# The experts' ranking, in ten steps between the first blocks' work, behind the gates of the first quad

## The chip, the cores and the metric

The kernel runs on one core of a Trainium2 chip. The metric is the device time of one execution, in microseconds (us); lower is better. The engines of a core are named as in the profile: PE (TensorE, matrix products; PEld is its loading of the stationary operand), DVE (VectorE), ACT (ScalarE), POOL (GpSimd) and SP (SyncE, which here issues the loads of weights). Each engine works through a row of instructions of its own, in a fixed order, and waits on semaphores for what others produce.

## The reference

Two layers of a small diffusion transformer, then a last block. Each of the two layers has a mixer (convolutions in layer 0, attention in layer 1), and then a mixture of 32 experts, over 512 tokens in layer 0 and 256 in layer 1. What matters here is the mixture:

```python
def hier_moe(tokens, w1, b1, w2, b2, w_gate, w_up, w_down):
    n = tokens.shape[0]
    p1 = jax.nn.softmax((tokens @ w1 + b1).astype(jnp.float32), axis=-1)
    p_grp, grp = lax.top_k(p1, 1)                       # one of 4 groups
    lg2 = (tokens @ w2 + b2).astype(jnp.float32).reshape(n, N_GROUPS, EXPERTS_PER_GROUP)
    lg2 = jnp.take_along_axis(lg2, grp[:, :, None], axis=1)[:, 0]
    top_val, top_idx = lax.top_k(lg2, TOP_K_INNER)      # two of its 8 experts
    gate = p_grp * jax.nn.softmax(top_val, axis=-1)
    expert = grp * EXPERTS_PER_GROUP + top_idx
    return grouped_experts(tokens, expert, gate.astype(tokens.dtype), w_gate, w_up, w_down)
```

`grouped_experts` computes, for each token and each of its two experts e, `(silu(x @ w_gate[e]) * (x @ w_up[e])) @ w_down[e]`, scales it with the gate and adds it to the token. The model width is 1024, an expert's hidden width 512, all in float32: an expert has three matrices of 2 MB.

## The kernel before

**Slots and blocks.** Every expert gets a block of slots for its tokens (64 slots, or with two blocks of 32 more for the experts with most tokens). The plan of blocks is fixed when the kernel is built; which expert takes which place in it is found out as the kernel runs. The first four experts (`FIX`) keep their fixed places. The other 28 are ranked by their number of tokens in `order` (L1464). Two blocks of 64 slots make a pair (128 slots), two pairs a quad (256 slots); layer 0 has 7 quads, layer 1 has 5.

**`order`** is a chain of operations on DVE alone, over arrays of 28 x 28 on all 128 partitions: comparing the counts, summing to ranks, then (L1499) casting `rows`, the row numbers in memory of the 28 experts in their rank order; then the places (`base`, `place`, `cap`, `rest`), then each token's slot (`slots`), and at its end `gB`, the gate weights by place for all quads but the first. The first quad's gate weights `gA` don't depend on it. Its scratch memory shares a buffer with `ysb`, the output of the blocks' down products (tag "ysb", one buffer).

**The stream of weights.** SP issues the loads in one order into a ring of slots. A slot is filled again when PE has finished with what was in it. The fixed experts' loads stand at L298; those of ranked experts at L309, and ahead of each ranked gate matrix SP reads the expert's row number from `rows` (L305).

**The work on a quad.** `new` and `onehot` make the matrix OH that says which token is in which slot; `dispatch` collects the tokens of a quad into `xs` (products with OH into a PSUM tile `pd`). `gates(q)` multiplies OH with `gA` or `gB`, so that each slot has its gate weight, as four products per pair in layer 0 (two halves each in the trace's count) into one `pd` tile; DVE copies the columns that matter into `gs`. There are two PSUM buffers for `pd`. Then for each block `hidden` (32 products for gate and up, ACT's Silu and DVE's `g<-acc,gs,g`, which takes the gate weight `gs`), `turn` (PE transposes `g` into `pt`), `down` (products with the down matrix into `acc`, then ACT and DVE write `ysb`), and per pair `spread` (products `pd<-OT,ysb` and DVE's addition to `res`).

**The order of work.** Everything is put into a queue with a lead of two jobs, so that a job's products stand on PE two jobs ahead of its elementwise work. Each job taken from the queue also advances background work (`self.bg`), a list of generators that run a step at a time between the jobs; `blocks`, which counts overflowing blocks, is such a one (by `slowly`). `job` puts a function into the queue. In the program before, `order` ran in one piece where it is called, ahead of the first `hidden`, and the queued `gates(0)` partly ahead of it and partly behind.

Of the kernel before, what the change touches and what calls it, by code (L numbers as in the profile page):

```python
# [138 lines left out]
class Kernel:  # L139
# [18 lines left out]
    def build_stream(self):  # L158
# [29 lines left out]
        def experts(l):  # L188
# [6 lines left out]
            ends.append(len(st))  # L195

        experts(0)
        mod(ada[1], [1])
        aw = I["attn_w_in"][0]
# [8 lines left out]
        for h in range(2):  # L208
# [3 lines left out]
                       [(slice(0, P), slice(4, 8), kp(aw[512:1024], h * 512, 512))]))  # L212
        mod(ada[1], [5])
        experts(1)
        mod(wm, [0, 1])
        w2 = I["w_in_2"][0]
# [1247 lines left out]
    def order(self, ep, l, T, rt):  # L1464

        nc = self.nc
        n = NE - FIX
        tmp = ep.tile([P, 2048], F32, tag="ysb", bufs=1, name="order")  # L1470
        o = [0]

        def part(n):
            o[0] += n
            return tmp[:, o[0] - n:o[0]]

        def square(v):
            return v.rearrange("p (a b) -> p a b", a=n)

        def along(v):  # L1480
            return v.unsqueeze(1).to_broadcast([P, n, n])

        def across(v):
            return v.unsqueeze(2).to_broadcast([P, n, n])

        E, w = part(n * n), part(n * n)
        key, rank, f = (part(n) for _ in range(3))
        base, place, cap, u = (part(NE) for _ in range(4))
        io, cnt, rest = self.c("iota"), rt["cnt"], rt["rest"]
        ranks, bases = (rt["plan"][:, 256 + i * n:256 + (i + 1) * n] for i in range(2))  # L1490
        self.stt(key, cnt[:, FIX:NE], float(NE), io[:, 0:n], OP.mult, OP.subtract)
        self.tt(square(w), along(key), across(key), OP.is_gt)
        nc.vector.tensor_reduce(out=rank, in_=square(w), axis=AX.X, op=OP.add)

        self.tt(square(E), across(ranks), along(rank), OP.is_equal)
        self.tt(square(w), square(E), along(io[:, 0:n]), OP.mult)
        nc.vector.tensor_reduce(out=f, in_=square(w), axis=AX.X, op=OP.add)
        self.ts(f, f, float(P), OP.mult, float((l * NE + FIX) * P), OP.add)
        nc.vector.tensor_copy(rt["rows"][:, 0:n], f)  # L1499
        self.ext[l] = rt["rows"]  # L1500
        self.st_fill()

        ET = E.rearrange("p (a b) -> p b a", a=n)
        self.tt(square(w), ET, along(bases), OP.mult)
        nc.vector.tensor_reduce(out=base[:, FIX:NE], in_=square(w), axis=AX.X, op=OP.add)
        self.tt(square(w), ET, along(io[:, FIX:NE]), OP.mult)
        nc.vector.tensor_reduce(out=place[:, FIX:NE], in_=square(w), axis=AX.X, op=OP.add)
        self.ts(base[:, 0:FIX], io[:, 0:FIX], float(SLOTS), OP.mult)
        nc.vector.tensor_copy(place[:, 0:FIX], io[:, 0:FIX])
        m32, m64 = PLANS[l].more  # L1510
        self.ts(cap, io[:, 0:NE], 0.0, OP.mult, float(SLOTS), OP.add)
        c = cap[:, FIX:NE]
        self.ts(c, rank, float(m32), OP.is_lt, 32.0, OP.mult)
        self.ts(u[:, 0:n], rank, float(m64), OP.is_lt, 32.0, OP.mult)
        self.stt(c, c, 32.0, u[:, 0:n], OP.add, OP.add)
        self.tt(rest, cnt, cap, OP.subtract)

        T2 = 2 * T
        oh, tm, eq = (w[:, i * T2 * NE:(i + 1) * T2 * NE].rearrange("p (t n) -> p t n", t=T2) for i in range(3))
        v = part(T * NE).rearrange("p (t n) -> p t n", t=T)  # L1520
        pl = part(T2)
        fi, wts = (rt[k].rearrange("p i t -> p (i t)") for k in ("fi", "wts"))
        self.tt(oh, io[:, 0:NE].unsqueeze(1).to_broadcast([P, T2, NE]), fi.unsqueeze(2).to_broadcast([P, T2, NE]),
                OP.is_equal)
        self.tt(v, rt["posm"], cap.unsqueeze(1).to_broadcast([P, T, NE]), OP.is_ge)
        self.stt(v, v, 65536.0, rt["posm"], OP.mult, OP.add)
        self.tt(v, v, base.unsqueeze(1).to_broadcast([P, T, NE]), OP.add)
        for i in range(2):
            ts = slice(i * T, (i + 1) * T)
            self.tt(tm[:, ts], oh[:, ts], v, OP.mult)  # L1530
        nc.vector.tensor_reduce(out=rt["slots"], in_=tm, axis=AX.X, op=OP.add)
        self.tt(tm, oh, place.unsqueeze(1).to_broadcast([P, T2, NE]), OP.mult)
        nc.vector.tensor_reduce(out=pl, in_=tm, axis=AX.X, op=OP.add)
        self.tt(eq, io[:, 0:NE].unsqueeze(1).to_broadcast([P, T2, NE]), pl.unsqueeze(2).to_broadcast([P, T2, NE]),
                OP.is_equal)
        self.tt(tm, eq, wts.unsqueeze(2).to_broadcast([P, T2, NE]), OP.mult)
        self.tt(rt["gB"], tm[:, 0:T], tm[:, T:T2], OP.add)

    def blocks(self, ep, l, T, rt):

        nc = self.nc

        nbt = ep.tile([P, NE], F32, name="nbt")
        nbf = ep.tile([P, 2 * T], F32, name="nbf")
        for j in range(2 * T):
            self.ts(nbt, rt["rest"], float(j * SLOTS), OP.is_gt)
            nc.vector.tensor_reduce(out=nbf[:, j:j + 1], in_=nbt, axis=AX.X, op=OP.add)
            if j % 2:
                yield
        nc.vector.tensor_reduce(out=nbt[:, 0:1], in_=nbf, axis=AX.X, op=OP.add)  # L1550
        nc.vector.tensor_copy(rt["nb"], nbt[:, 0:1])

    def experts(self, ep, mp, l, T, hhl, rt):
# [8 lines left out]
        B = plan.blocks  # L1562
        NB = len(B)
        npair = (plan.slots + P - 1) // P
        nq = (plan.slots + 255) // 256
        pairs = [[i for i in range(NB) if B[i][1] // P == p] for p in range(npair)]
# [67 lines left out]
        def down(b):  # L1634

            e, off, m, first, last = B[b]
            us = slice(off % P, off % P + m)
            c = D * m // P

            def pe(k, n):  # L1640
                if k == 0:
                    st["y"] = self.acc()
                a = st["y"]
                w, num = st["wd", e]
                hT = st["hT", b].rearrange("p (k s) -> p k s", k=4)
                for i in range(k, k + n):
                    for j in range(P // m):
                        self.mm(a[j * m:(j + 1) * m, 0:c], hT[:, i], w[:, i, j * c:(j + 1) * c], i == 0, i == 3)
                if k + n == 4:
                    if last:  # L1650
                        self.done(num)
                    out(a)

            def out(a):
                if off % P == 0:
                    st["ysb"] = ep.tile([P, 2, D], F32R, tag="ysb", bufs=1, name="ysb")
                H, L = (st["ysb"][us, i] for i in range(2))

                H, L = (v.rearrange("s (k p) -> s k p", k=8) for v in (H, L))
                for ps in (lo, hi) if m == 64 else quarters:  # L1660
                    self.parts(H[:, :, ps], L[:, :, ps], a[ps, 0:c].rearrange("s (p k) -> s k p", k=8))

            return [(None, lambda _, a=a: pe(*a)) for a in (((0, 2), (2, 2)) if m == 64 else ((0, 4),))]

        def slots(p):

            return min(P, plan.slots - p * P)

        def gates(q):

            src = rt["gB" if q else "gA"]
            pd = self.pd()
            gs = st["gs", q] = ep.tile([P, 8], F32, tag="gs", bufs=2, name="gs")
            for p in range(2 * q, min(2 * q + 2, npair)):
                r, m = p % 2, slots(p)
                e0, e1 = B[pairs[p][0]][0], B[pairs[p][-1]][0] + 1
                for t in range(T):
                    self.mm(pd[0:m, 8 * r:8 * r + e1 - e0], self.OH[:, t, r * P:r * P + m].bitcast(F32),
                            src[:, t, e0:e1], t == 0, t == T - 1)
                for b in pairs[p]:  # L1680
                    e, off, m, _, _ = B[b]
                    c = 8 * r + e - e0
                    for i in range(P // m):
                        nc.vector.tensor_copy(gs[i * m:(i + 1) * m, nth[b]:nth[b] + 1],
                                              pd[off % P:off % P + m, c:c + 1])
# [43 lines left out]
        def job(f, *a):  # L1729
            self.push(None, lambda _: f(*a))  # L1730
# [17 lines left out]
        for p in range(npair):  # L1748
            o, q = at[pairs[p][0]], p // 2
# [24 lines left out]
        new(0)  # L1774
        for k in (0, 2, 4, 6):
            dispatch(st["xs", 0], k, 0, False)
        job(gates, 0)
        self.order(ep, l, T, rt)
        self.bg.append(self.slowly(self.blocks(ep, l, T, rt), 20, 1))
        for b in range(NB):  # L1780
            if l and B[b][0] == TABLES and B[b][3]:
# [1142 lines left out]
```

## Time and profile before

| | us |
|---|---|
| median of 3 runs | 1979.12 |
| lowest and highest run | 1971.8, 1981.99 |
| the profiled execution | 1978.93 |
| its span in the trace | 1977.2 |

The span is the part of the execution that the hardware profiler saw; what lies around it is 1.7 us. Mean granted clock of TensorE over the span: 0.922 of full speed, where 1 is 2.4 GHz. A row of the profile gives the start in us from the span's start, the duration, the engine, the line of the kernel, the operation, the tiles (out<-in), and in brackets the idle time of the engine just before with what released it.

### The profile page before, as it was taken

The page shows a single profiled execution, that of the slowest core. Times are in us where ns is not written, and L with a number is a line of the kernel's source. Part 1 is how long each engine was busy: PE and PEld are TensorE (multiplying, and loading weights), DVE is VectorE, ACT ScalarE, POOL GpSimd, SP SyncE. Part 2 cuts the span into 40 slices and gives each one's busy share as a digit, 9 for nine tenths or more (in the row PEclk, how much of TensorE's full clock was granted, in tenths as well). Part 3 has the DMA queues.
Part 4 walks back from the last instruction along what each step waited for, and adds up shares of the span by engine and source line. Part 5 has one row for each costly group of instructions (what it writes and reads, how often), then busy time and mean ns, then how long its engine had stood idle before and what let it go on. Part 6 is the DMA issues. An engine that isn't in the chain of part 4 may idle for free.

```text
span 1977.2 us, 41036 instructions
## 1 busy us (share of the span) xinstructions
PE 1676.6 (85%) x17718; PEld 1265.6 (64%) x17718; DVE 1037.5 (52%) x2368; ACT 585.3 (30%) x1140; POOL 108.4 (5%) x171
## 2 busy tenths in 40 slices
PE   6999959889989897998959985666655898999997
PEld 4866746555565555785645554445443887879997
DVE  2898673444343444646672342263643656575455
ACT  3223231112112112525521211212112524655443
POOL 2011110000000000204100001000000000000000
PEclk8999979899999999999979997878878899999999
DMA  9465538799999999955348899999999334587530
GB/s 349 170 214 180 213 147 370 324 370 421 425 393 423 414 427 402 320 148 169 143 176 335 366 426 396 425 426 426 426 426 364 122 130 171 208 294 284 206 128 22
DMA packets 116922, 582.34 MB, mean 295 GB/s; under 512 B 9836, under 2 KB 14480, under 8 KB 92160
## 3 DMA queue, kind: packets, MB, share of 16 engines
q1 hardware_dynamic: 108896, 569.16, 72.8%
q0 software_dynamic: 6368, 10.27, 1.9%
q8 instruction: 141, 2.31, 0.5%
q10 hardware_dynamic: 1472, 0.23, 0.1%
q14 instruction: 45, 0.37, 0.1%
HBM read 578.47 MB, written 1.16 MB: 293 GB/s over the span
## 4 chain that ended last, share of the span: by engine, by line
PE 61%; DMA 18%; DVE 14%; ACT 4%; issue 2%; SPq 0%; DVEq 0%; ACTq 0%
PE acc L472 42%; PE pd L472 16%; DMA w<-in_expert_w_gate_dram 9%; DMA w<-in_expert_w_up_dram 5%; DMA w<-in_ada_w_dram 3%; PE pt L476 2%; DVE ya L498 1%; ACT x L2134 1%; DVE L L489 1%; DVE m L2129 1%; DMA w<-in_w_in_dram 1%; DVE ysb L489 1%; DVE order L489 1%; PE pt L472 1%; ACT ysb L486 1%
## 5 line engine op out<-in xcount | busy, mean ns | idle before, releaser
L489 DVE TENSOR_TENSOR L<-w,H 128x1024 fp32r<-128x1024 f32 (+2 forms) x173 | 205.8, 1195 | 155.7 <-ACT H L486 155.0
L472 PE MATMUL acc<-w,xs 128*32 128x128 f32 (+1 forms) x3776 | 192.0, 342 | 107.3 <-DMA w<-in_expert_w_gate_dram 73.6
L472 PEld LDWEIGHTS acc<-w,xs 128*32 128x32 f32 (+1 forms) x3776 | 151.7, 137 | 148.0 <-issue 76.8
L489 DVE TENSOR_TENSOR ysb<-acc,ysb 32x256 fp32r<-32x256 f32 (+1 forms) x218 | 105.2, 482 | 223.1 <-ACT ysb L486 222.8
L486 ACT ACTIVATE H<-w 128x1024 fp32r<-128x1024 f32 (+2 forms) x174 | 178.3, 1033 | 105.2 <-PE acc L472 89.0
L472 PE MATMUL acc<-w,x 128*32 128x128 f32 (+1 forms) x3200 | 204.3, 319 | 0.2 <-DMA w<-in_expert_w_gate_dram 0.2
L486 ACT ACTIVATE ysb<-acc 32x256 fp32r<-32x256 f32 (+1 forms) x218 | 92.6, 425 | 356.3 <-PE acc L472 250.5
L472 PE MATMUL acc<-w,hT 128*32 128x256 f32 (+1 forms) x1744 | 189.7, 467 | 3.3 <-issue 3.3
L472 PEld LDWEIGHTS acc<-w,x 128*32 128x32 f32 (+1 forms) x3200 | 136.5, 122 | 73.2 <-issue 40.3
L498 DVE SCALAR_TENSOR_TENSOR g<-acc,gs,g 128x128 f32<-128x128 f32 (+1 forms) x67 | 26.7, 398 | 218.8 <-ACT g L486 218.7
L472 PE MATMUL pd<-OT,ysb 128*128 128x512 f32 (+1 forms) x384 | 102.9, 379 | 37.6 <-ACT ysb L486 16.3
L472 PEld LDWEIGHTS acc<-w,hT 128*32 128x32 f32 (+1 forms) x1744 | 72.2, 125 | 89.1 <-issue 66.8
L498 DVE SCALAR_TENSOR_TENSOR res<-pd,modc,res 128x256 f32<-128x256 f32 x208 | 88.0, 476 | 69.8 <-PE pd L472 68.4
L486 ACT ACTIVATE g<-acc 128x128 f32<-128x128 f32 (+1 forms) x67 | 21.3, 318 | 279.4 <-PE acc L472 279.4
L472 PEld LDWEIGHTS pd<-OT,ysb 128*128 128x128 f32 x384 | 59.1, 199 | 68.9 <-ACT ysb L486 21.2
L472 PE MATMUL pd<-uh,H 128*128 128x256 f32 x352 | 99.8, 283 | 0.7 <-ACT modrow L486 0.7
L472 PE MATMUL pd<-uh,L 128*128 128x256 f32 x352 | 99.7, 283 | 0.0
L472 PE MATMUL pd<-ul,H 128*128 128x256 f32 x352 | 99.6, 283 | 0.0
L693 POOL DMA_DIRECT2D modd<-modrow x42 | 24.4, 583 | 1228.5 <-ACT modrow L486 1177.5
L472 PE MATMUL pd<-w,cc 128*32 128x128 f32 (+1 forms) x2016 | 78.3, 306 | 14.2 <-DMA w<-in_ada_w_dram 7.6
L472 PE MATMUL pd<-OH,hhl 128*128 128x256 f32 (+1 forms) x608 | 86.4, 295 | 3.1 <-DVE OH L489 1.7
L472 PEld LDWEIGHTS pd<-OH,hhl 128*128 128x128 f32 x608 | 77.8, 197 | 13.6 <-issue 10.8
(510 smaller groups left out, 3137.0 us busy)
## 6 DMA issues: line engine op xcount, KB each, us to landing
w<-in_expert_w_gate_dram SPq DMA_DIRECT2D x64, 2048.0 KB, 18.0
w<-in_expert_w_up_dram SPq DMA_DIRECT2D x64, 2048.0 KB, 16.7
w<-in_expert_w_down_dram SPq DMA_DIRECT2D x64, 2048.0 KB, 16.3
w<-in_ada_w_dram SPq DMA_DIRECT2D x24, 2048.0 KB, 14.5
w<-in_w_mod_dram SPq DMA_DIRECT2D x12, 2048.0 KB, 10.7
w<-in_w_in_dram SPq DMA_DIRECT2D x6, 2048.0 KB, 9.0
w<-in_conv_w_in_dram SPq DMA_DIRECT2D x5, 2048.0 KB, 20.8
w<-in_w_ffn_gate_dram SPq DMA_DIRECT2D x5, 2048.0 KB, 9.3
```

The lines of the kernel that those rows point to most:

```text
L472: self.nc.tensor.matmul(out, lhsT, rhs, start=start, stop=stop)
L476: self.nc.tensor.transpose(out, in_, self.c("ident")[0:n, 0:n])
L486: self.nc.scalar.activation(out, in_, f, **kw)
L489: self.nc.vector.tensor_tensor(out=out, in0=a, in1=b, op=op)
L498: self.nc.vector.scalar_tensor_tensor(out=out, in0=a, scalar=s, in1=b, op0=op0, op1=op1)
L693: nc.gpsimd.dma_start(d[i].rearrange("(j c) -> j c", j=4), row[r:P:32])
L2129: nc.vector.tensor_reduce(out=m[:, u:u + 1], in_=s, axis=AX.X, op=OP.max)
L2134: nc.scalar.activation(p, s, AF.Exp, scale=0.125, bias=m[:, u:u + 1], accum_out=su[:, u:u + 1])
```

## The change

`order` becomes a generator with nine yields, that is ten steps, and is put on the list of background work ahead of `blocks`. `gates(0)` is called directly ahead of it. In `gates` the copies form a loop of their own, behind the products of both pairs. `rt["ordered"]` is set at the end of `order`, and an assertion in `out` (while the program is built) makes sure that `ysb` is taken only after it.

```diff
@@ order @@
         self.tt(square(w), along(key), across(key), OP.is_gt)
         nc.vector.tensor_reduce(out=rank, in_=square(w), axis=AX.X, op=OP.add)
+        yield
 
         self.tt(square(E), across(ranks), along(rank), OP.is_equal)
         self.tt(square(w), square(E), along(io[:, 0:n]), OP.mult)
+        yield
         nc.vector.tensor_reduce(out=f, in_=square(w), axis=AX.X, op=OP.add)
         self.ts(f, f, float(P), OP.mult, float((l * NE + FIX) * P), OP.add)
         nc.vector.tensor_copy(rt["rows"][:, 0:n], f)
         self.ext[l] = rt["rows"]
         self.st_fill()
+        yield
 
         ET = E.rearrange("p (a b) -> p b a", a=n)
         self.tt(square(w), ET, along(bases), OP.mult)
         nc.vector.tensor_reduce(out=base[:, FIX:NE], in_=square(w), axis=AX.X, op=OP.add)
+        yield
...
         self.tt(rt["gB"], tm[:, 0:T], tm[:, T:T2], OP.add)
+        rt["ordered"] = True
@@ out @@
             def out(a):
+                assert "ordered" in rt
@@ gates @@
                 for t in range(T):
                     self.mm(pd[0:m, 8 * r:8 * r + e1 - e0], self.OH[:, t, r * P:r * P + m].bitcast(F32),
                             src[:, t, e0:e1], t == 0, t == T - 1)
+            for p in range(2 * q, min(2 * q + 2, npair)):
                 for b in pairs[p]:
                     e, off, m, _, _ = B[b]
-                    c = 8 * r + e - e0
+                    c = 8 * (p % 2) + e - B[pairs[p][0]][0]
@@ experts @@
-        job(gates, 0)
-        self.order(ep, l, T, rt)
+        gates(0)
+        self.bg.append(self.order(ep, l, T, rt))
         self.bg.append(self.slowly(self.blocks(ep, l, T, rt), 20, 1))
```

Five more yields stand in the part of `order` that is left out.

What moves on the engines. First PE's row at layer 0's first quad, with its waits on DVE's semaphore: the last of the dispatch, the gate products and the first products of block 0. Before:

```order
L472 MATMUL pd<-OH,hhl 128x256 x15
L472 MATMUL pd<-gA,OH 128x2 [waits DVE_49]
L472 MATMUL pd<-gA,OH 128x2 x3
L472 MATMUL pd<-gA,OH 128x2 [waits DVE_49]
L472 MATMUL pd<-gA,OH 128x2 x3
L472 MATMUL acc<-w,x 64x256 [waits DMAHW5_49]
```

And now:

```order
L472 MATMUL pd<-OH,hhl 128x256 x15
L472 MATMUL pd<-gA,OH 128x2 [waits DVE_49]
L472 MATMUL pd<-gA,OH 128x2 x7
L472 MATMUL acc<-w,x 64x256 [waits DMAHW5_49]
```

The order of the products is the same; the second pair's wait for DVE is gone. Second, DVE's row at the same place (difference; the line numbers after L1491 shift because of the new lines): the copies of the gates and the begin of `order`.

```order
 L498 SCALAR_TENSOR_TENSOR gA<-oh,wts,gA 128x32
 L481 COPY x<-pd 128x512 x2
+L1695 COPY gs<-pd 64x1 x8
 L498 SCALAR_TENSOR_TENSOR order<-cnt,csb 128x28
 L489 TENSOR_TENSOR order<-order 128x784
```

The eight copies now stand ahead of the ranking's first instruction. Third, further down in DVE's row, where the first block's product `g` has moved to, between the fourth and the fifth step:

```order
 L489 TENSOR_TENSOR order<-order,plan 128x784
-L1505 TENSOR_REDUCE order<-order 128x28
+L1508 TENSOR_REDUCE order<-order 128x28
+L498 SCALAR_TENSOR_TENSOR g<-acc,gs,g 128x256
 L489 TENSOR_TENSOR order<-order,csb 128x784
-L1507 TENSOR_REDUCE order<-order 128x28
+L1511 TENSOR_REDUCE order<-order 128x28
 L493 TENSOR_SCALAR order<-csb 128x4
```

L1505 and L1508 are one instruction, the last of the fourth step. And the end of the ranking on DVE:

```order
 L489 TENSOR_TENSOR order<-order,wts 128x256
 L489 TENSOR_TENSOR gB<-order 128x128
-L1684 COPY gs<-pd 64x1 x8
-L498 SCALAR_TENSOR_TENSOR g<-acc,gs,g 128x256 x2
+L498 SCALAR_TENSOR_TENSOR g<-acc,gs,g 128x256
 L489 TENSOR_TENSOR ysb<-acc,ysb 64x8x64 x2
```

Where the copies and two products `g` stood, only the second product is left. The rows of PE, ACT, POOL and SP keep their order everywhere; some waits on DVE that another wait had covered are now written out, among them one of ACT's first `ysb<-acc` for the end of `order`.

## Rows read from the trace of the kernel before

**Rows 1.** The page, part 1: busy us, share of span, instructions.

```profile
PE 1676.6 (85%) x17718; PEld 1265.6 (64%) x17718; DVE 1037.5 (52%) x2368; ACT 585.3 (30%) x1140; POOL 108.4 (5%) x171
```

**Rows 2.** PE's waits, whole span: us in total, times, longest.

```profile
PE acc L472 <- DMA w<-in_expert_w_gate_dram: 73.8, 18, 9.5
PE pd L472 <- DVE gs L1684: 48.6, 12, 14.7
```

**Rows 3.** Timeline, layer 0's first quad: start, duration, engine, line, operation.

```profile
275.83 0.18 DVE L498 SCALAR_TENSOR_TENSOR order<-cnt,csb 128x28 f32<-128x28 f32 x1
...
276.92 0.95 PE L472 MATMUL pd<-gA,OH 128*128 128x2 f32 x8
...
281.29 0.18 DVE L1499 CAST rows<-order 128x28 int32<-128x28 f32 x1
...
283.00 0.97 DVE L1505 TENSOR_REDUCE order<-order 128x28 f32<-128x784 f32 x1
...
291.60 0.29 DVE L489 TENSOR_TENSOR gB<-order 128x128 f32<-128x128 f32 x1
...
292.54 1.87 PE L472 MATMUL pd<-gA,OH 128*128 128x2 f32 x8 [14.67 <-DVE gs L1684]
...
305.60 0.48 DVE L498 SCALAR_TENSOR_TENSOR g<-acc,gs,g 128x256 f32<-128x256 f32 x1 [10.49 <-ACT g L486]
...
308.52 0.66 PE L476 MATMUL pt<-csb,g 128*64 128x128 f32 x4
...
316.26 0.59 ACT L486 ACTIVATE ysb<-acc 64x512 fp32r<-64x512 f32 x1 [3.05 <-PE acc L472]
...
319.71 0.36 SPq L309 DMA_DIRECT2D w<-in_expert_w_gate_dram  x1
```

**Rows 4.** Windows, layer 0: us, busy PE PEld DVE ACT POOL, PEclk, DMA, GB/s.

```profile
275.00:280.00 5.00, 2.87 (x26) 2.78 (x24) 4.63 (x6) 0.60 (x1) 0.58 (x1) 0.98 0.82 347
277.00:292.50 15.50, 0.87 (x9) 0.78 (x7) 14.71 (x34) 0.60 (x1) 0.00 (x0) 0.59 0.13 56
295.00:300.00 5.00, 5.00 (x28) 2.73 (x26) 0.11 (x1) 0.00 (x0) 0.00 (x0) 0.50 0.00 0
436.00:510.00 74.00, 66.49 (x746) 42.89 (x738) 31.96 (x90) 13.55 (x33) 0.00 (x0) 0.95 1.00 418
```

**Rows 5.** Chain of waits: start, us, what; 32 products of a block, three times.

```profile
294.41 6.54 PE acc L472 x32
...
320.69 3.60 PE acc L472 x32
...
1040.86 5.38 PE acc L472 x32
```

**Rows 6.** Timeline, layer 1's first quad.

```profile
1024.64 0.50 PE L472 MATMUL pd<-gA,OH 128*128 128x2 f32 x4
...
1039.85 1.01 PE L472 MATMUL pd<-gA,OH 128*128 128x2 f32 x4 [14.71 <-DVE gs L1684]
...
1053.59 0.65 PE L476 MATMUL pt<-csb,g 128*64 128x128 f32 x4
...
1061.33 0.36 SPq L309 DMA_DIRECT2D w<-in_expert_w_gate_dram  x1
```

**Rows 7.** Windows, layer 1: the pause, and a stretch with the second quad's gates.

```profile
1024.50:1039.80 15.30, 0.64 (x7) 0.55 (x5) 14.48 (x35) 0.60 (x1) 0.00 (x0) 0.59 0.00 1
1086.00:1120.00 34.00, 31.75 (x333) 18.40 (x332) 12.19 (x39) 5.90 (x13) 0.00 (x0) 0.90 0.83 337
```

**Rows 8.** PE's waits between 280 and 800 us.

```profile
PE pd L472 <- DVE gs L1684: 23.5, 7, 14.7
```

**Rows 9.** Timeline, second quad's gates in layer 0, then in layer 1.

```profile
350.08 1.72 DVE L1684 COPY gs<-pd 64x1 f32<-64x1 f32 x10
...
351.85 1.87 PE L472 MATMUL pd<-gB,OH 128*128 128x2 f32 x8 [1.81 <-DVE gs L1684]
...
1089.08 1.02 PE L472 MATMUL pd<-gB,OH 128*128 128x3 f32 x4 [2.08 <-DVE gs L1684]
```

More of the change, by code (lines that the diff above doesn't have):

```diff
@@ L1516, in order @@
         self.tt(rest, cnt, cap, OP.subtract)
+        yield
         T2 = 2 * T
@@ L1527, in order @@
         self.tt(v, v, base.unsqueeze(1).to_broadcast([P, T, NE]), OP.add)
+        yield
         for i in range(2):
@@ L1531, in order @@
         nc.vector.tensor_reduce(out=rt["slots"], in_=tm, axis=AX.X, op=OP.add)
+        yield
         self.tt(tm, oh, place.unsqueeze(1).to_broadcast([P, T2, NE]), OP.mult)
         nc.vector.tensor_reduce(out=pl, in_=tm, axis=AX.X, op=OP.add)
+        yield
         self.tt(eq, io[:, 0:NE].unsqueeze(1).to_broadcast([P, T2, NE]), pl.unsqueeze(2).to_broadcast([P, T2, NE]),
```

## The prediction

> **What bounds the kernel now.** The page's first part comes first: TensorE (PE) is busy for 1676.6 of 1977.2 us [rows 1], so the reader looks next at what fills the rest. The waits of PE over the whole span [rows 2] say it: weight loads are the largest entry (73.8 us), and the second is 48.6 us in 12 waits on "DVE gs L1684", the copies of the gates. The longest of these is 14.7 us, so I looked for where it lies. The timeline of layer 0's first quad [rows 3] shows it: the first pair's eight gate products run at 276.92, the second pair's eight come at 292.54, 14.67 us later. Yet the copies they wait for are short: ten take 1.72 us [rows 9]. VectorE (DVE) is in `order`, from 275.83 to 291.89; the copies stand behind it in DVE's row. The pause is thus the ranking, under the copies' name. Layer 1 shows the same [rows 6]: 14.71 us.
>
> The windows [rows 4, 7] add two things. In both pauses the loads stand still as well (56 and 1 GB/s, against 418 GB/s in 436 to 510 us): the ring is full, and a slot comes free only when PE has used it. And the granted clock falls: 0.98 before layer 0's pause, 0.50 (the 1.2 GHz level) after it, until block 0's first products are over. The chain of waits [rows 5] gives the price: the 32 products at 294.41 take 6.54 us, the same 32 take 3.60 at 320.69.
>
> **What the change moves.** PE's, ScalarE's and SP's orders stay; only DVE's differs. The eight gate copies of quad 0 now stand ahead of `order`, and `order` is cut into ten steps with the blocks' work between. In every quad the copies come after both pairs' products, so the second pair's products no longer wait for the first pair's copies: they fall in another part of the same PSUM tile, and the row of PE has no wait there any more.
>
> *Front of layer 0.* The first pair's products end at 276.92+0.95 = 277.87. The second pair's follow at once and, at the full clock, take another 0.95 instead of 1.87. Saved: 14.67 for the pause, 0.92 for that group, and 6.54−3.60 = 2.94 for block 0's first 32 products, if the clock now stays up. That is 18.5. The clock's share (3.9) is not shown by any row of before; its bounds are 0 and 3.9. I take 3.9, since in 275 to 280, before the idle time, the clock was 0.98 at 2.87 us of PE work in 5.
>
> *Front of layer 1.* 14.71, and 1.01−0.50 = 0.51 for the second group, and 5.38−3.60 = 1.78 for the 32 products: 17.0, of which 2.3 hangs on the clock.
>
> *Later quads.* In layer 0 PE waited 23.5 us for copies between 280 and 800 us [rows 8]; without the first pause 8.8. Of this 1.81 is quad 1's [rows 9], and 7.0 is left for the others, where the change takes the wait out. In quad 1 the twenty copies now stand in one block after the products, and the second spread job, which needs the same one of two PSUM buffers, waits for all of them where it waited for the second ten: up to 1.72 later. So 1.81+0.92 (the second group at the full clock, as at the front) is gained and 1.72 lost: 1.0, or 3.9 if the block behind it then keeps the full clock too, as at the front (2.9). I take 1.5, near the lower end, since three microseconds without products remain there. For the other quads of layer 0 the loads decide: the DMA share is already 1.00 at 418 GB/s in 436 to 510, and PE can't run ahead of its weights. The 7.0 is worth between 0 and 7.0; I take 3, since [rows 4] speak for 0 and [rows 8] for 7.0. In layer 1, quad 1 waits 2.08, and loses up to another 2.3 to the clock as the front did; 1086 to 1120 has a DMA share of 0.83, so this counts: 2.1 to 4.4, I take 3.5. Its later quads lie where PE waits for loads (the 73.8 of [rows 2]): 0. In sum 8.0, between 3.1 and 15.3.
>
> The Trainium skill's page "DMA: Bandwidth & Descriptors", section "Where 436 GB/s comes from", says that between HBM and SBUF the HBM side binds, at about 358 GB/s a core. The 418 GB/s here disagrees, and the measurement decides; by the page's figure the loads would be the bound of every later quad, the third term would be 0 and the sum 35.5.
>
> *What the ten steps cost.* The instructions are the same in number and size, so nothing is added on DVE; what matters is what stands behind each now. Three readers could be late.
> - Row numbers (SP reads them for the first ranked load, 319.71). Products end near 278.8, the eight copies near 280.4, and `order` starts there instead of at 275.83, 4.6 us later. Rows were ready at 281.47, so now at 286.0. SP needs them at 319.71−18.5 = 301.2: 15 us of slack. In layer 1 `order` starts near 1027.2, rows are ready at 1032.8, and are needed at 1061.33−17.0 = 1044.3.
> - Block 0's `g` product (DVE, after the fourth step). Four steps took 275.83 to 283.97, 8.14 us; from 280.4 they end at 288.5 and the product at 289.0. PE wants it at 308.52−18.5 = 290.0: 1.0 us of slack. ScalarE's half is ready at 305.60−18.5 = 287.1, so the product is late by 1.4 against what it could be, hidden by PE's own products. In layer 1: 1035.8 against 1053.59−17.0 = 1036.6.
> - The end of `order`: 16.06 us of work and a 0.48 product from 280.4 is 296.9; `ysb` shares its scratch, and ScalarE wants it at 316.26−18.5 = 297.8, 0.9 later.
> All three cost 0 by this, but the last two have only about 1 us of cover; without it each microsecond of lateness is one on PE.
>
> *Does the shift last?* Loads are released by PE freeing slots, nothing here is set to a fixed time, and the ring is full at both pauses; so all that follows comes earlier by the same amount, the loads too.
>
> **Sum.** 18.5+17.0+8.0 = 43.5. The profiled execution took 1978.93 (span 1977.2), 0.2 less than the median of the three runs, 1979.12. Forecast: 1978.93−43.5 = 1935.4, say 1936. Own range: 1978.93−35.5−3.1 = 1940 to 1978.93−35.5−15.3 = 1928; the three runs of before spread by −7 and +3 us about their median.
>
> **Rivals.**
> - *Only the fronts pay*; the quads' waits are taken up by loads. For it: DMA share 1.00. Against: 0.83 behind layer 1's front. 1978.93−35.5 = 1943.4.
> - *The clock does not come back*: it falls behind the dispatch though the pause is gone. For it: 0.90 in 1086 to 1120, where PE is busy for 31.75 of 34 us. Against: 0.98 in 275 to 280. Only the pauses count, 14.67+14.71 = 29.4: 1949.6.
> - *The stall moves to the `g` product.* If ranking steps pass ahead of it, TensorE stands at the turn of block 0. The 1.0 us of cover is thin. The remaining steps last 291.89−283.97 = 7.9 us, so at worst, with the cover off, 6.9 us in each layer: 43.5−13.8 = 29.7, or 1949. The Trainium skill's page "PSUM — Partial Sum Buffer", section "Engine vs sequencer instructions", says that VectorE's queue is strictly first in, first out. By that rule a ready product can't pass a ranking step, as the copies couldn't in [rows 3]; the trace agrees with its 14.67 us.
> - *The loads take back a front*: transfers that began early run into the next full stretch and PE waits there instead. One layer's gain lost: 1978.93−18.5 = 1960.
> - *Slower: SP stands at the row number.* If the rows came after their slot, SP, which issues every load in order, would stop, and all loads behind it. With rows later by d than worked out in both layers, this costs (d−15.2)+(d−11.5): it eats the gain of 43.5 at d = 35, and at d = 40 the time is 1978.93−43.5+53.3 = 1989. Nothing in the steps' lengths supports that: the whole of `order` is 16 us.
> - *It does nothing*: PE waits for loads right behind each pause instead. Against it: the stream is idle in both pauses. 1979.
>
> **How the numbers follow.** Forecast 0.66; only the fronts 0.15; clock not returned 0.07; stall at the `g` product 0.05; a front taken back 0.03; nothing 0.02; slower 0.02. From 1928 less half of that spread, 1924, to 1953, beyond the cases at 1950, holds the first four, less their outer parts: about 8 to 9 in 10. Half a per cent (10 us) is about what a measurement of this kernel tells from none; all but the last two cases are faster by more than that: 0.96, 0.02 and 0.02.
>
> **What would show it.** Right: one run of PE's gate products without a gap in both layers; a granted clock near 1 from 277 to 300; the first ranked load near 301 in layer 0, and in layer 1 near 1061.3−18.5−17.0−4.5 = 1021 (the 4.5 from layer 0's later quads); no PE wait of over 3 us on the copies; `order` in pieces on DVE between 280 and 297. Wrong: PE waiting for "DVE g" at the first turn, for ScalarE's first `ysb`, or a larger sum of waits on the gate loads, 73.8 now, which would mean that the gain was taken back by the stream.

## The result and the profile after

The changed kernel takes 1928.6 us in the median (1926.76 to 1931.71, 4 runs) beside 1975.46 for the kernel before on the same chip: a ratio of 0.9757, with a 95% interval of 0.9731 to 0.9783. In a later series it was 0.9765 [0.9741, 0.9789]. That is 46 to 48 us. One of the later series' six executions took 5356 us and isn't in its ratio, and nothing here shows why. The profiled execution took 1927.27 us with a span of 1925.5, 51.7 less than before: one trace each, in which the one of before lies in the upper half of its runs and the one of after in the lower half.

The page, its first line and part 1:

```profile
span 1925.5 us, 41039 instructions
...
PE 1657.2 (86%) x17718; PEld 1258.7 (65%) x17718; DVE 1038.0 (54%) x2368; ACT 585.1 (30%) x1140; POOL 108.4 (6%) x171
```

DVE is as busy as before [rows 1]: its work moved, and none of it went. PE's busy time fell by 19.4 us with the same number of instructions: the same products ran more often at the full clock, whose mean rose from 0.922 to 0.938.

PE's waits over the whole span:

```profile
PE acc L472 <- DMA w<-in_expert_w_gate_dram: 102.3, 24, 7.8
PE acc L472 <- DMA w<-in_expert_w_up_dram: 20.6, 16, 2.2
```

The 48.6 us for the copies of the gates [rows 2] have left the top of the list, and the waits for the gate matrices grew from 73.8 to 102.3. Part of what the copies no longer take, the loads do; how much of that is a loss is worked out behind the experiments. Over the whole span the copies have one entry left:

```profile
PE pd L472 <- DVE gs L1695: 3.0, 1, 3.0
```

The timeline of layer 0's first quad, which answers to [rows 3]:

```profile
276.56 1.84 PE L472 MATMUL pd<-gA,OH 128*128 128x2 f32 x16
...
278.34 3.67 PE L472 MATMUL acc<-w,x 128*64 128x256 f32 x32
...
278.44 1.34 DVE L1695 COPY gs<-pd 64x1 f32<-64x1 f32 x8 [2.88 <-PE pd L472]
...
279.80 0.19 DVE L498 SCALAR_TENSOR_TENSOR order<-cnt,csb 128x28 f32<-128x28 f32 x1
...
285.28 0.18 DVE L1501 CAST rows<-order 128x28 int32<-128x28 f32 x1
...
286.25 0.39 ACT L486 ACTIVATE g<-acc 128x256 f32<-128x256 f32 x1 [2.89 <-PE acc L472]
...
287.05 0.97 DVE L1508 TENSOR_REDUCE order<-order 128x28 f32<-128x784 f32 x1
288.05 0.48 DVE L498 SCALAR_TENSOR_TENSOR g<-acc,gs,g 128x256 f32<-128x256 f32 x1
...
289.59 0.65 PE L476 MATMUL pt<-csb,g 128*64 128x128 f32 x4
...
296.10 0.29 DVE L489 TENSOR_TENSOR gB<-order 128x128 f32<-128x128 f32 x1
...
297.32 0.59 ACT L486 ACTIVATE ysb<-acc 64x512 fp32r<-64x512 f32 x1 [3.05 <-PE acc L472]
```

The sixteen gate products run without a gap, and the first 32 products of block 0 follow in 3.67 us. DVE copies first and ranks from 279.80. `g` is ready 1.06 us before PE takes it, `order` ends 0.93 us before ACT wants `ysb`, and PE and ACT wait for neither. The windows of the two fronts (columns as in [rows 4]) show a full PE at the full clock where [rows 4, 7] had a pause:

```profile
277.00:292.50 15.50, 15.50 (x139) 10.48 (x140) 13.50 (x30) 2.10 (x5) 0.38 (x1) 1.00 0.79 302
295.00:300.00 5.00, 5.00 (x40) 2.63 (x38) 3.07 (x8) 1.19 (x2) 0.00 (x0) 1.00 1.01 433
997.00:1012.00 15.00, 15.00 (x136) 9.77 (x137) 13.78 (x32) 1.90 (x5) 0.00 (x0) 1.00 0.65 241
```

SP's queue has the first ranked loads in layer 0 at 300.77 and in layer 1 at 1016.25, where [rows 3, 6] had 319.71 and 1061.33.

Where the gain arises can be read from the loads, since a load is issued when PE frees its slot. How much earlier than in the trace of before the same load is issued, in us (the down matrices are numbered over both layers):

| load of | behind | after | again | first quads only | layer 0 only | layer 1 only |
|---|---|---|---|---|---|---|
| down 5 | layer 0's front | 18.9 | 17.6 | 19.0 | 18.0 | −0.2 |
| down 6 | its second quad | 20.7 | 20.3 | 18.9 | 19.0 | 0.8 |
| down 24 | its fifth | 27.8 | 25.0 | 20.8 | 25.1 | 3.0 |
| down 32 | layer 0's last load | 22.4 | 19.6 | 16.5 | 20.0 | 0.8 |
| down 34 | ahead of layer 1's front | 26.4 | 19.3 | 19.2 | 19.9 | 1.4 |
| down 36 | layer 1's front | 45.1 | 37.3 | 36.1 | 20.0 | 18.2 |
| down 38 | ahead of its second quad's gates | 45.0 | 37.3 | 36.0 | 19.9 | 18.2 |
| down 40 | its second quad | 50.4 | 42.6 | 36.0 | 21.5 | 23.5 |
| down 64 | the last expert | 50.4 | 42.5 | 35.6 | 22.1 | 23.5 |
| span | | 51.7 | 41.6 | 35.7 | 23.1 | 25.1 |

"Again" is a second trace of the changed kernel; the last three are experiments. The two traces of one kernel differ most between the layers (+4.0 and −0.3 from down 32 to down 34): what differs there is no part of the change.

The shifts in the table also hold what differs ahead of a front: the gate products of layer 0 begin at 276.92 us before [rows 3], at 276.56 after and at 277.87 in the second trace. A front's own gain is the time from its first gate product to the load behind it (down 5, down 36). For layer 0, one line of before, one of after and two of the second trace (the first gate products of the others are shown above):

```profile
330.01 0.33 SPq L309 DMA_DIRECT2D w<-in_expert_w_down_dram  x1
...
311.07 0.33 SPq L309 DMA_DIRECT2D w<-in_expert_w_down_dram  x1
...
277.87 1.84 PE L472 MATMUL pd<-gA,OH 128*128 128x2 f32 x16
...
312.37 0.33 SPq L309 DMA_DIRECT2D w<-in_expert_w_down_dram  x1
```

That is 53.09 us before and 34.51 and 34.50 after: 18.6 us gained in both traces. For layer 1, whose gate products begin at 1024.64 before [rows 6], one line of before and two of after:

```profile
1069.19 0.33 SPq L309 DMA_DIRECT2D w<-in_expert_w_down_dram  x1
...
996.59 0.97 PE L472 MATMUL pd<-gA,OH 128*128 128x2 f32 x8
...
1024.11 0.33 SPq L309 DMA_DIRECT2D w<-in_expert_w_down_dram  x1
```

44.55 us before and 27.52 after: 17.0 gained, and the same in the second trace (1004.38 to 1031.89).

### The profile page after: what moved, and what is told of

Read it like the earlier page. It is cut to its first block, busy times and chain, and to the rows that moved or that the text cites. A ratio compares the mean times of both kernels' runs of the same rounds, so it can differ in the third digit from the quotient of the medians.

```text
span 1925.5 us, 41039 instructions
## 1 busy us (share of the span) xinstructions
PE 1657.2 (86%) x17718; PEld 1258.7 (65%) x17718; DVE 1038.0 (54%) x2368; ACT 585.1 (30%) x1140; POOL 108.4 (6%) x171
## 4 chain that ended last, share of the span: by engine, by line
PE 61%; DMA 20%; DVE 12%; ACT 4%; issue 2%; SPq 1%; DVEq 0%; ACTq 0%
PE acc L472 42%; PE pd L472 16%; DMA w<-in_expert_w_gate_dram 11%; DMA w<-in_expert_w_up_dram 5%; PE pt L476 2%; DVE ya L498 1%; ACT x L2145 1%; DMA w<-in_w_in_dram 1%; DMA w<-in_ada_w_dram 1%; DVE L L489 1%; DVE m L2140 1%; DVE ysb L489 1%; ACT ysb L486 1%; DMA modd<-modrow 1%; SPq L298 1%
## 5 line engine op out<-in xcount | busy, mean ns | idle before, releaser
L472 PE MATMUL acc<-w,xs 128*32 128x128 f32 (+1 forms) x3776 | 195.1, 348 | 113.3 <-DMA w<-in_expert_w_gate_dram 92.5
L472 PE MATMUL acc<-w,hT 128*32 128x256 f32 (+1 forms) x1744 | 179.0, 442 | 2.4 <-issue 2.4
## 6 DMA issues: line engine op xcount, KB each, us to landing
w<-in_expert_w_gate_dram SPq DMA_DIRECT2D x64, 2048.0 KB, 19.2
w<-in_conv_w_in_dram SPq DMA_DIRECT2D x5, 2048.0 KB, 20.3
```

The costliest lines, as they stand in the source:

```text
L472: self.nc.tensor.matmul(out, lhsT, rhs, start=start, stop=stop)
```

## Experiments

**The copies behind the products, alone** (`c_copies`):

```diff
 # before, with after's gates(); job(gates, 0) and the one-piece order stay
+            for p in range(2 * q, min(2 * q + 2, npair)):
                 for b in pairs[p]:
                     e, off, m, _, _ = B[b]
-                    c = 8 * r + e - e0
+                    c = 8 * (p % 2) + e - B[pairs[p][0]][0]
```

> Before, with only the copies put behind all products of a quad; the ranking stays in one piece ahead of the copies on DVE. If the lateness of what TensorE waits for decides, the pause before the second pair goes, and TensorE runs on until it wants block 0's g: that comes at 291.9 (end of the ranking) + 1.4 (copies) + 0.5 = 293.8 against 290.0, a new wait on DVE g of 3.8 us, and 4.4 us in layer 1. Fronts 18.5+17.0-8.2 = 27.3, later quads as in the changed kernel 12.5 (7.2 and 5.3 by the load issues of the two traces): span about 1977-40 = 1937. Rival, that the gates must stand ahead of the ranking: most of the two pauses returns at the g products, span 1955 or more. Rival, that taking PE's wait away is all: 1926, as the changed kernel.

Ratio 0.9839 [0.9813, 0.9865], span 1944.1, 7 us over what was expected. The new waits came as expected, 3.9 and 4.3 us (PE's waits over the span):

```profile
PE pt L476 <- DVE g L498: 8.2, 2, 4.3
```

What was missing at the fronts is the clock: it fell during these waits (0.50 from 294.6 to 296.6), and the 32 products behind the first took 4.65 us instead of 3.67, those behind the second 5.10. With the turns ahead of them this is 3.0 us of the 7. Most of the rest is that the expectation put 7.2 on layer 0's later quads, from one trace; here they gain 3.5 (from down 5 to down 32). Moving PE's wait to a later point where PE has 12 us of other work gave about two thirds of the gain. So the pause wasn't only DVE's ranking; it was also how little work PE had ahead of it.

**Gates first, ranking in one piece** (`cg_onepiece`):

```diff
 # c_copies, and
-        job(gates, 0)
+        gates(0)
         self.order(ep, l, T, rt)
```

> The changed kernel without the yields: gates and their copies first, then the ranking in one piece. By DVE's order block 0's g comes behind 16.1 us of ranking that now starts at 279.8: 296.3 against 289.6 (changed kernel), a wait of 6.7 us on DVE g, and in layer 1 6.0. Fronts 36-12.7 = 23.3, later quads 12.5: span about 1977-36 = 1941, slower than the copies alone. Rival, that the steps are not needed since TensorE has enough other work: 1926.

Ratio 0.986 [0.9835, 0.9886], span 1946.3. PE waited 7.0 and 5.9 us for `g`, as expected from DVE's order; the timeline of layer 0's PE (start, duration, engine, operation, idle time before):

```profile
298.05 1.04 PE L476 MATMUL pt<-csb,g 128*64 128x128 f32 x4 [6.98 <-DVE g L498]
...
299.02 5.90 PE L472 MATMUL acc<-w,x 128*64 128x256 f32 x32
```

Again the products behind ran at the lower level (granted clock 0.50 from 298.1 to 303), which the expectation had left out; with it the span is 5 us above 1941. By spans this is 2 us behind the copies alone, in the direction expected, but the intervals overlap, so the time doesn't show that order; the rows of the two fronts do (18.2 us gained here, 24.3 with the copies alone, counted from the first gate products). That both lose to the changed kernel is shown by the time: without the steps, putting the gates first only moves the stall to `g`.

**The steps, without the copies' new place** (`s_split`):

```diff
 # after, with before's gates(), and
-        gates(0)
+        job(gates, 0)
         self.bg.append(self.order(ep, l, T, rt))
```

> The ranking in ten steps as background work, gates queued as before and copied per pair as before. The copies then stand ahead of the ranking by the queue alone; block 0's g stands behind the fifth step. Second pair waits about 1.9 us for the copies, g comes at about 292.5 against 291.5: 1 to 2 us. Fronts 36-2x3.5 = 29, later quads 0: span about 1948. Rival, that the copies' place is what counts: 1965 or more.

Ratio 0.9843 [0.982, 0.9867], span 1941.9, 6 us under what was expected. The second pair waited 0.8 us instead of 1.9, and for `g`, here behind the fifth step, PE waited 2.0 and 2.1. Behind the second of these waits, in layer 1, the clock fell. PE in layer 0, then in layer 1, and a window in layer 1:

```profile
292.58 0.63 PE L476 MATMUL pt<-csb,g 128*64 128x128 f32 x4 [1.96 <-DVE g L498]
293.14 3.67 PE L472 MATMUL acc<-w,x 128*64 128x256 f32 x32
...
1017.86 0.65 PE L476 MATMUL pt<-csb,g 128*64 128x128 f32 x4 [2.11 <-DVE g L498]
1018.44 5.36 PE L472 MATMUL acc<-w,xs 128*64 128x256 f32 x32
```

```profile
1019.90:1021.90 2.00, 2.00 (x14) 1.06 (x12) 0.92 (x4) 0.00 (x0) 0.00 (x0) 0.50 1.00 426
```

From the first gate products on, the two fronts gain 15.7 and 12.2 us here, 27.8 of the changed kernel's 35.6. The queue alone puts the copies ahead of the ranking once that is background work; what the direct call of `gates(0)` does is to place `g` one step earlier. The call was not tried by itself.

**The later quads left as they were** (`q0_only`):

```diff
 # after, and in gates()
-            for p in range(2 * q, min(2 * q + 2, npair)):
-                for b in pairs[p]: (copies)
+                if q:                  # copies(): the loop of copies as a function
+                    copies([p])        # inside the loop of products
+            if not q:
+                copies(range(min(2, npair)))
```

> The changed kernel with the copies behind all products in the first quad alone, per pair in the later ones. If the fronts are 36 of the 51.7 us and the later quads the rest, the span is about 1941. Rival, that the loads give back or take any change of the later quads: 1926 to 1930.

Ratio 0.9812 [0.9786, 0.9837], span 1941.5: the fronts by themselves are worth 35.7 us of the span. In the table the second quad of layer 1 gains nothing here (36.0 to 36.0, from down 38 to down 40) and 5.3 to 5.4 in every trace with its copies moved. The quads behind layer 0's front lose 2.5 by its last load, where the changed kernel gains 3.5 and 2.0; these are single traces, and two of one kernel differ by 1.5 there.

**One layer alone** (`layer0`, `layer1`):

```diff
+        if l == 0:      # layer1: l == 1; late is the same test, in gates()
             gates(0)
             self.bg.append(self.order(ep, l, T, rt))
+        else:
+            job(gates, 0)
+            for _ in self.order(ep, l, T, rt):
+                pass
```

> All of the change in layer 0 alone. The load issues of the two traces stand 26.1 us apart at the end of layer 0. If this lasts to the end: span about 1977-26 = 1951. Rival, that layer 1's loads take it back: 1965 or more.

> All of the change in layer 1 alone: 17.1 for the front, 5.3 for the second quad, 0 to 1.3 behind: span about 1953.5. With the run of layer 0 alone the two gains should add up to 51.7. Rival, that the loads bind layer 1: under 17.

Layer 0 alone: 0.9878 [0.985, 0.9905], span 1954.1. Layer 1 alone: 0.9907 [0.9885, 0.993], span 1952.1. The gains in the spans, 23.1 and 25.1, add up to 48.2; those of the ratios, 1.22% and 0.93%, to 2.15% beside 2.4% for both. 48.2 is 3.5 under the 51.7 expected, and 51.7 itself is one trace; the second has 41.6. Layer 0's gain lasts through all of layer 1 (19.9 to 22.1 in the table), so the loads don't take a front back.

**More work ahead of `g`** (`extra4`, `extra2`): the ranking's first comparison, whose result is written again unchanged, five or three times.

```diff
-        self.tt(square(w), along(key), across(key), OP.is_gt)
+        for _ in range(5):      # extra2: 3
+            self.tt(square(w), along(key), across(key), OP.is_gt)
```

> The changed kernel with the first comparison of the ranking done five times instead of once: 3.9 us more on DVE ahead of block 0's g in each layer. If the cover is 1.1 us in layer 0 (289.59 less 288.53) and 0.9 in layer 1, TensorE waits 2.8 and 3.0 us for DVE g: 5.8 us slower, and up to 2 more behind the first ysb; span about 1932. Rival, that the ranking is off the path with room to spare: same time, 1926.

Ratio 0.9821 [0.9795, 0.9847], span 1935.2. One span against another can't tell here, since the changed kernel's two are 1925.5 and 1935.6; the ratios stand 11 to 13 us apart. Counted from the first gate products, the fronts are 5.9 and 4.7 us slower than the changed kernel's, 10.6 together and not 6 to 8. The waits are those expected, 3.0 and 3.1 us, but behind them PE ran at the lower level of the clock. The timeline of PE in layer 0, and the window behind the wait:

```profile
292.57 1.04 PE L476 MATMUL pt<-csb,g 128*64 128x128 f32 x4 [3.00 <-DVE g L498]
...
293.54 6.13 PE L472 MATMUL acc<-w,x 128*64 128x256 f32 x32
```

```profile
292.60:297.60 5.00, 5.00 (x24) 2.83 (x26) 4.76 (x15) 0.75 (x2) 0.00 (x0) 0.50 1.02 436
```

3.00 of wait, 1.04−0.65 = 0.4 and 6.13−3.67 = 2.5: 5.9 us for 3.9 us of DVE work with 1.0 us of cover. In layer 1 it is 3.1, 0.4 and 4.74−3.67 = 1.1. So the smaller dose was run:

> Two more comparisons ahead of block 0's g instead of four, 1.95 us per layer. The cover of 1.0 us leaves a wait of 1.0 us on DVE g in layer 0 and 1.1 in layer 1. If the granted clock falls at any wait, block 0's second half is slow as with four (32 products in about 6 us) and the time is 6 to 8 us above the changed kernel; if a wait of that size leaves the clock up (32 products in 3.67), it is 2 us above.

Ratio 0.9779 [0.9759, 0.98] beside 0.9765 for the changed kernel in the same series: the 2 us expected are too little to be seen there, 6 to 8 would put it near 0.980. The trace decides:

```profile
294.40 0.63 PE L476 MATMUL pt<-csb,g 128*64 128x128 f32 x4 [1.02 <-DVE g L498]
...
294.96 3.67 PE L472 MATMUL acc<-w,x 128*64 128x256 f32 x32
```

The wait is 1.02 us, and the clock stays up: 3.67 us. In layer 1 it is 1.17, and 3.67 again. The cover of 1 us is real; waits of about 1 us cost their own length, those of 3 us one and a half times and twice theirs.

**The changed kernel again, and the gates' tile elsewhere** (`after_again`, `acc_tile`, `acc_tile_5`):

```diff
-            pd = self.pd()
+            pd = self.acc() if q else self.pd()
             gs = st["gs", q] = ...
```

> The changed kernel with the gates' PSUM tile of the later quads from the pool of the expert products (four buffers) instead of the two of the spread jobs. If the 3.0 us that TensorE waits for DVE gs in the second quad come from the shared pair of buffers, they go, and what is gained in layer 0 is taken back by the loads in part: 0 to 6 us below the changed kernel, span 1920 to 1926. Rival: the four buffers are all in use, and block products wait for the copies instead: same or slower.

> The changed kernel once more, as the measure for the two others on the same chip: 0.976 of before.

> The gates' tile of later quads from the pool of four, against the changed kernel in more rounds. The first trace moved the second quad of layer 0 forward by 5.5 us and layer 0's end by 3, and ended 3.5 us earlier. If that is real: 0.974, 2 to 4 us under the changed kernel. Rival, that the loads take it all back: equal.

The new tile gave 0.9742 [0.9719, 0.9766], and 0.9747 [0.9726, 0.9769] beside 0.9765 [0.9741, 0.9789] for the changed kernel: some 3 us, in both series the same way, but within the intervals. It does in the trace what it should. The changed kernel in layer 0's second quad:

```profile
331.85 0.71 PE L472 MATMUL pd<-OT,ysb 128*128 128x512 f32 x2
...
332.02 3.42 DVE L1695 COPY gs<-pd 64x1 f32<-64x1 f32 x20 [0.97 <-PE pd L472]
...
335.59 1.19 PE L472 MATMUL pd<-OT,ysb 128*128 128x512 f32 x2 [3.04 <-DVE gs L1695]
...
336.71 5.48 PE L472 MATMUL acc<-w,hT 128*64 128x512 f32 x16
```

and the same place with the tile from the pool of four:

```profile
331.94 1.16 PE L472 MATMUL pd<-OT,ysb 128*128 128x512 f32 x4
...
332.12 3.42 DVE L1695 COPY gs<-acc 64x1 f32<-64x1 f32 x20 [0.97 <-PE acc L472]
...
333.03 3.65 PE L472 MATMUL acc<-w,hT 128*64 128x512 f32 x16
```

The two spread jobs follow each other, the clock stays, and down 6 is issued 26.2 and 25.1 us earlier than before instead of 20.7 and 20.3. At layer 0's last load it is 27.2 and 28.7 against 22.4 and 19.6. Most of it lasts there; how much of it reaches the end, these runs can't tell.

## Why the prediction was right

The time fell by 46 to 48 us where 43.5 were forecast; by the interval of the ratio the gain is 43 to 53. The fronts came out by the mechanism described, to a tenth of a microsecond; that the third term's sum fits is partly luck. The time itself, 1928.6, is 6.8 below the forecast of 1935.4 and 0.6 above the range's lower end. 3.5 of this is the start: the forecast counted down from one execution at 1978.93, and the kernel before has a median of 1975.46 here. Step by step:

- *The pauses are the ranking under the copies' name.* Right. With the steps they are gone, and in the one-piece ranking they come back under another name, `g`, with the length that DVE's order gives (7.0 and 5.9 us). The Trainium skill's page "PSUM — Partial Sum Buffer", section "Engine vs sequencer instructions", has VectorE's queue as strictly first in, first out; both waits agree with it.
- *Front of layer 0, 18.5.* 18.6, counted from the first gate product, in both traces of the changed kernel and in the two experiments that leave this front as it is (first quads only, layer 0 only). The 17.6 to 19.0 of the table hold what lies ahead of the front.
- *Front of layer 1, 17.0.* 17.0, counted in the same way, in both traces and in the two experiments (first quads only, layer 1 only).
- *The clock's share, 3.9 and 2.3, which no row of before could show.* Right: the 32 products behind the gates took 3.67 us in both layers, where [rows 5] have 6.54 and 5.38. And it is the clock and no cover by chance: where a wait of 3 us or more came back, the level of 0.50 and the long products came back with it.
- *The stream follows.* Right; layer 0's gain alone is still there at the last expert. But the loads do set a limit inside layer 0. In the changed kernel PE is 27.8 us ahead at down 24 and only 22.4 at down 32, with a wait of 7.8 us for a gate matrix in between that the kernel before didn't have; from 664 to 734 us its loads run at 426 GB/s with a DMA share of 1.01.
- *The sign of being wrong that came.* A larger sum of waits on the gate loads was to mean that the stream had taken the gain back, and the sum rose by 28.5 us, from 73.8 to 102.3. Most of that rise is no gain taken back. In layer 1 (1040 to 1510 us) two lines of before, then one of after:

```profile
PE acc L472 <- DMA w<-in_expert_w_gate_dram: 73.6, 17, 9.5
...
PE acc L472 <- ACT ysb L486: 11.3, 2, 6.2
...
PE acc L472 <- DMA w<-in_expert_w_gate_dram: 92.5, 22, 7.8
```

  The two waits on "ACT ysb" end at 1311.18 and 1430.71 us; gate matrices land at 1311.05 and 1430.57, within 0.1 us of ACT's end, so the loads alone would have held PE as long. Counted with them, layer 1 has 7.6 us more of load waits (92.5−73.6−11.3), and there the copies of the later quads no longer take 8.3 (25.1−14.7−2.08): loads in place of copies, which the prediction put at 0, and the table's shift stays at 50.4 from down 40 to down 64. The other 9.6 us lie in layer 0 (0.2 before, 9.8 after), and there the loads did take back part of the gain. The fronts themselves were not taken back. The other sign, no wait of over 3 us on the copies, was just missed at 3.04.
- *Later quads, 8.0.* The sum fits, at 8.9 and 7.4, but by two errors that offset each other. In layer 1's second quad the forecast was 3.5, at most 4.4; it is 5.3 to 5.4 in each of the nine traces that move its copies, and 0.0 to 1.6 in the three others with a changed front or layer 0. The working had 2.08 for the wait and took the clock's part from the front. What falls away is 2.08, and 5.88−3.65 = 2.2 in the down products, and about 1.1 in the gate group and the first spread job, which ran at the lower level as well. Two lines of before, behind the wait [rows 9], then three of after:

```profile
1089.96 1.20 PE L472 MATMUL pd<-OT,ysb 128*128 128x256 f32 x4
1091.09 5.88 PE L472 MATMUL acc<-w,hT 128*64 128x512 f32 x16
...
1041.36 1.05 PE L472 MATMUL pd<-gB,OH 128*128 128x2 f32 x8
...
1042.28 0.72 PE L472 MATMUL pd<-OT,ysb 128*128 128x256 f32 x4
...
1042.93 3.65 PE L472 MATMUL acc<-w,hT 128*64 128x512 f32 x16
```

  Layer 0's quads were put at 4.5 (1.5 and 3). The changed kernel gains 3.5 and 2.0 there, less than forecast. The second quad's own part, put at 1.0 to 3.9, is 1.8 and 2.7 (20.7−18.9, 20.3−17.6), so the quads behind it, put at 3, gave 1.7 and −0.7. (With the copies of the later quads left as they were, 2.5 are lost there, so the move itself may be worth 4.5 to 6; this rests on single traces.) The wait of all twenty copies was forecast and came, 3.04 us.
- *The three readers.* Rows were ready at 285.46 (forecast 286.0) and read at 300.77 (301.2); `g` had 1.06 us of cover (forecast 1.0); `order` ended 0.93 us ahead of `ysb` (0.9). (The listing of the change has eight yields, so nine steps, one fewer than the text beside it counts; no term used the number.) That the cover was real and thin, the doses show: 1.95 us more on DVE made a wait of 1.0, 3.9 us one of 3.0.
- *The rivals.* "Only the fronts", 1943.4, is the time of the experiment that leaves the later quads out (1943.23 in the profiled execution, 1941.71 in the median); the changed kernel lies below it. "The stall moves to g" is what happens without the steps. SP never stood at the row number; its late case was not tried.

The sum of the three terms as measured in two traces is 44.5 and 43.0 (18.6, 17.0 and 8.9 or 7.4), beside 43.5. The spans fell by 51.7 and 41.6; what is over or missing lies mostly between and behind the layers, where the kernels are the same, and the difference between the two spans is larger than the third term. That part stays unexplained.

## What to carry to other kernels

A wait is booked under the last instruction that releases it; what counts is all that stands ahead of that instruction in its engine's row, and moving the instruction ahead of the long work, or cutting the long work into steps, are worth the same only if the next reader in line isn't caught behind it. So for every piece moved, reckon when the next reader wants its result, and how much cover that leaves: here a cover of 1 us stood between nothing and 5 to 6 us a layer. Where the second reader of a two-buffer pool waits for slow copies out of the first tile, giving that tile another pool can take the wait away, as it did here for 3.04 us.

## What had not been expected of the hardware

A short wait of PE can cost its own length or much more. At one place, ahead of block 0's turn, the experiments made ten waits of PE for `g`; the clock is the granted one while the 32 products behind run, at its lowest:

| run, layer | wait, us | clock | 32 products, us |
|---|---|---|---|
| `extra2`, 0 | 1.02 | 1.00 | 3.67 |
| `extra2`, 1 | 1.17 | 1.00 | 3.67 |
| `s_split`, 0 | 1.96 | 1.00 | 3.67 |
| `s_split`, 1 | 2.11 | 0.50 | 5.36 |
| `extra4`, 0 | 3.00 | 0.50 | 6.13 |
| `extra4`, 1 | 3.13 | 0.50 | 4.74 |
| `c_copies`, 0 | 3.91 | 0.50 | 4.65 |
| `c_copies`, 1 | 4.33 | 0.50 | 5.10 |
| `cg_onepiece`, 1 | 5.92 | 0.50 | 5.03 |
| `cg_onepiece`, 0 | 6.98 | 0.50 | 5.90 |

In these rows the price behind a wait doesn't grow with its length. Waits of 1.96 and 2.11 us stand on either side here, and in the second quads of before waits of 1.81 and 2.08 us [rows 9] went with the lower level. The window from the end of the wait of 1.81 on, in the kernel before (PEclk is the third number from the end):

```profile
351.80:355.00 3.20, 2.93 (x10) 2.21 (x10) 1.15 (x8) 0.00 (x0) 0.00 (x0) 0.50 1.00 430
```

So these runs give no safe length, and what decides they don't settle. An extra 2 us at a front is too little for the times of this kernel, whose runs spread by 10 us, while the trace shows it to a tenth: compare such steps by rows of the trace, counted from a row close ahead of them, and use the time for the sum.
